# Channel shuffle on one core: eleven tiles of up to 51 KB a partition in two load and two store buffers, in place of fifteen tiles of up to 38 KB in two and three

## The chip, the cores and the metric

The kernel runs on one core of one Trainium2 chip. The metric is the device time of one execution in microseconds. The core has a VectorE (DVE) that copies data inside the on-chip memory (SBUF, 128 partitions), two sequencers that issue transfers here (SP for loads, ACT for stores), and 16 DMA engines that carry them out. The time before is the median of three runs, which lie between 316.12 and 316.22 us.

## The reference

The input x has the shape 16 x 64 x 64 x 256 in float32, 67.1 MB. The 256 channels are 8 groups of 32, and the two channel axes change places at each pixel:

```python
x = x.reshape(batch, h, w, groups, channels_per_group)
x = x.transpose(0, 1, 2, 4, 3)
x = x.reshape(batch, h, w, c)
```

No value is changed. Each pixel's 256 floats (1 KB) are permuted within that kilobyte, so any cut of the data between pixels is allowed.

## The kernel before

All 65,536 pixels lie in one line in memory. A tile is a run of 128 x q pixels: partition p of the tile holds q neighbouring pixels, so q KB a partition, and in DRAM the tile is one contiguous block. The list `_SLOTS` (line 12) gives the tiles' q in order: a tile of 12 that is loaded and stored in two parts of 4 and 8, one of 28, twelve of 38 and one of 16. They sum to 512 KB a partition.

For each tile three things happen. SP issues the load from DRAM into a buffer of the load pool (line 55). VectorE copies the buffer into one of the store pool, reading with a stride so that the channels are permuted (the copy of lines 57 to 60, L57 in the profile). ACT issues the store of that buffer to DRAM (line 61). A tile with two parts has two loads, two copies and two stores.

The order on each engine is the order in which the program is written (the schedule is set to manual in line 43); each engine goes through its own instructions one after another, and semaphores hold an instruction until what it needs is there. Both pools hand out their buffers in turn, each of the size of the largest tile. With two load buffers (line 13), a load waits until the copy of the tile two places back has ended. With three store buffers (line 14), a copy waits until the store of the tile three places back has landed, besides its own load. A store waits for its copy. Buffers take 2 x 38 + 3 x 38 = 190 KB of each partition.

Loads go through one DMA queue (q1 in the profile), stores through another (q10). Each DMA moves one contiguous piece of q KB for each partition, eight pieces on each of the 16 DMA engines.

Of the kernel before, what the change touches and what calls it, by code (L numbers as in the profile page):

```python
# [1 line left out]

# [4 lines left out]


F32 = mybir.dt.float32
P = 128  # L10

_SLOTS = [[4, 8], [28]] + [[38]] * 12 + [[16]]
_IN_BUFS = 2
_OUT_BUFS = 3


@with_exitstack
def kernel(
    ctx: ExitStack,
    tc: tile.TileContext,  # L20
    x: bass.AP,
    groups: bass.AP,
    out: bass.AP,
):
    nc = tc.nc
    b, h, w, c = x.shape
    G = int(groups)
    CPG = c // G
    assert G * CPG == c
    assert sum(map(sum, _SLOTS)) * P == b * h * w  # L30
    biggest = max(map(sum, _SLOTS))

    x_flat = x.rearrange("b h w c -> (b h w c)")
    out_flat = out.rearrange("b h w c -> (b h w c)")

    in_pool = ctx.enter_context(tc.tile_pool(name="in_pool", bufs=_IN_BUFS))
    out_pool = ctx.enter_context(tc.tile_pool(name="out_pool", bufs=_OUT_BUFS))

    def rows(flat, first, q):

        return flat[first * c : (first + P * q) * c].rearrange("(p f) -> p f", p=P)

    ctx.enter_context(tc.manual_schedule(engines=None))
    first = 0
    for parts in _SLOTS:
        in_tile = in_pool.tile([P, biggest * c], F32, name="in_tile")
        out_tile = out_pool.tile([P, biggest * c], F32, name="out_tile")
        at = 0
        pieces = []
        for q in parts:  # L50
            pieces.append((q, first, slice(at * c, (at + q) * c)))
            first += P * q
            at += q
        for q, start, cols in pieces:
            nc.sync.dma_start(out=in_tile[:, cols], in_=rows(x_flat, start, q))  # L55
        for q, start, cols in pieces:
            nc.vector.tensor_copy(  # L57
                out=out_tile[:, cols].rearrange("p (i j g) -> p i j g", j=CPG, g=G),
                in_=in_tile[:, cols].rearrange("p (i g j) -> p i j g", g=G, j=CPG),
            )  # L60
            nc.scalar.dma_start(
                out=rows(out_flat, start, q), in_=out_tile[:, cols]
            )


# [1 line left out]
_INS = ['x', 'groups']  # L67
_OUTS = [((16, 64, 64, 256), 'float32')]

_NUMBERS = {'groups': 8}  # L70


# [26 lines left out]
```

## Time and profile before

| what | value |
|---|---|
| median of three runs | 316.12 us |
| span of the profiled execution | 314.4 us |
| VectorE busy | 119.0 us in 16 copies |
| moved | 67.11 MB read, 67.11 MB written, mean 427 GB/s |
| copy of 38 KB a partition | 8.79 us mean, 12 of them |
| load of 38 KB a partition, issue to landing | 37.0 us median |
| store of 38 KB a partition, issue to landing | 42.6 us median |

A profile shows one execution, taken by the hardware profiler. Its own time, the span, runs from the first to the last instruction; the time of a run also contains what lies around that. The page gives busy times of the engines, then the span in 40 equal slices with the DMA engines' busy share in tenths and the GB/s moved; then the chain of waits that ended last, which is followed back from the last instruction to whatever released each step. Behind each group of instructions stands the idle time of its engine before them and what ended it. "DVE" is VectorE, "SPq" and "ACTq" are the sequencers that issue loads and stores. The latency of a DMA contains the time that it stands in its queue behind others: a 38 KB load moves 4.98 MB.

### The profile page before, as it was taken

What the parts mean: (1) busy time and instruction counts of PE and PEld (TensorE: products, weight loads), DVE (VectorE), ACT (ScalarE), POOL (GpSimd) and SP (SyncE); (2) the same over time, 40 slices, a digit from 0 to 9 for tenths busy, and PEclk for the clock granted to TensorE, in tenths of its full rate; (3) what the DMA queues carried; (4) which work ended last, traced back from release to release, by engine and by line L of the source; (5) the groups of instructions that cost most, each with busy time, mean ns of one, the idle gap of its engine ahead of it and who ended that gap; (6) DMA issues with size and microseconds to landing.
All of it is one profiled execution on the core that took longest, in us unless ns stands there. A gap on an engine that the chain in (4) does not pass through costs nothing.

```text
span 314.4 us, 132 instructions
## 1 busy us (share of the span) xinstructions
DVE 119.0 (38%) x16; POOL 0.2 (0%) x4
## 2 busy tenths in 40 slices
DVE  2081907309109109019028028037046055065400
POOL 0000000000000000000000000000000000000000
DMA  7999999999999999999999999999999999999997
GB/s 317 405 441 416 435 416 483 401 465 406 450 421 446 426 436 436 401 470 396 475 396 475 396 470 401 470 401 470 401 450 421 446 426 436 436 417 450 429 421 321
DMA packets 4608, 134.22 MB, mean 427 GB/s; under 512 B 512, under 2 KB 512, under 8 KB 768
## 3 DMA queue, kind: packets, MB, share of 16 engines
q1 hardware_dynamic: 2304, 67.11, 49.8%
q10 hardware_dynamic: 2304, 67.11, 49.4%
HBM read 67.11 MB, written 67.11 MB: 427 GB/s over the span
## 4 chain that ended last, share of the span: by engine, by line
DMA 76%; DVE 19%; issue 0%; SPq 0%; DVEq 0%
DMA in_tile<-in_x_dram 76%; DVE out_tile L57 19%; SPq L55 0%; DVEq L57 0%
## 5 line engine op out<-in xcount | busy, mean ns | idle before, releaser
L57 DVE COPY out_tile<-in_tile 128x9728 f32<-128x9728 f32 (+4 forms) x16 | 119.0, 7440 | 179.4 <-DMA in_tile<-in_x_dram 179.4
L80 POOL MEMSET const-uint8-127<- 128x1 uint8 x1 | 0.1, 103 | 0.0
L80 POOL MEMSET const-bfloat16-1.0<- 128x1 bf16 x1 | 0.1, 102 | 0.0
L80 POOL MEMSET const-float32-1.0<- 128x1 f32 x1 | 0.1, 100 | 0.0
L80 POOL MEMSET const-float32-0.0<- 128x1 f32 x1 | 0.1, 99 | 0.2 <-issue 0.2
## 6 DMA issues: line engine op xcount, KB each, us to landing
in_tile<-in_x_dram SPq DMA_DIRECT2D x12, 4864.0 KB, 37.0
out_dram<-out_tile ACTq DMA_DIRECT2D x12, 4864.0 KB, 42.6
in_tile<-in_x_dram SPq DMA_DIRECT2D x1, 3584.0 KB, 14.7
out_dram<-out_tile ACTq DMA_DIRECT2D x1, 3584.0 KB, 30.9
in_tile<-in_x_dram SPq DMA_DIRECT2D x1, 2048.0 KB, 30.4
out_dram<-out_tile ACTq DMA_DIRECT2D x1, 2048.0 KB, 15.2
in_tile<-in_x_dram SPq DMA_DIRECT2D x1, 1024.0 KB, 5.4
out_dram<-out_tile ACTq DMA_DIRECT2D x1, 1024.0 KB, 25.0
```

What stands on the lines that cost most here:

```text
L57: nc.vector.tensor_copy(out=out_tile[:, cols].rearrange("p (i j g) -> p i j g", j=CPG, g=G), in_=in_tile[:, cols].rearrange("p (i g j) -> ...
L80: nc = _bacc.Bacc("TRN2", target_bir_lowering=False, num_devices=1)
```

## The change

The list of tiles and the number of store buffers change: one tile of 20 KB a partition, nine of 51 KB and one of 33 KB, no tile in two parts, and two store buffers. The sum is again 512 KB. The buffers grow to 51 KB each, and the two pools take 2 x 51 + 2 x 51 = 204 KB of each partition. There are 11 loads, 11 copies and 11 stores in place of 16 each; a copy waits for the store of the tile two places back. Nothing else is touched.

```diff
-_SLOTS = [[4, 8], [28]] + [[38]] * 12 + [[16]]
+_SLOTS = [[20]] + [[51]] * 9 + [[33]]
 _IN_BUFS = 2
-_OUT_BUFS = 3
+_OUT_BUFS = 2
```

## The prediction

> **What bounds the kernel now.** I read the page first, then DMA shares in windows, the waits, the timeline and the single DMA packet records of the trace. The page:
>
> ```profile
> span 314.4 us, 132 instructions
> DVE 119.0 (38%) x16; POOL 0.2 (0%) x4
> ...
> DMA  7999999999999999999999999999999999999997
> ...
> DMA packets 4608, 134.22 MB, mean 427 GB/s; under 512 B 512, under 2 KB 512, under 8 KB 768
> ...
> DMA in_tile<-in_x_dram 76%; DVE out_tile L57 19%; SPq L55 0%; DVEq L57 0%
> ```
>
> The chain of waits (last line) calls loads 76% and copies 19% of the path. The DMA row above it says more: apart from the first and the last slice the 16 DMA engines are never idle. VectorE is busy for 38%. The chain runs load, copy, load, because a load is issued when a copy frees its buffer; but that load then waits behind another one. So the copies on the chain cost nothing as long as both queues, or at least one, hold work. The windows confirm it (columns: stretch, length, DVE busy, POOL busy, clock, DMA share, GB/s):
>
> ```profile
> 94.00:140.00 46.00, 17.54 (x2) 0.00 (x0) 1.00 1.00 433
> 140.00:186.00 46.00, 17.67 (x2) 0.00 (x0) 1.00 1.00 433
> 186.00:232.00 46.00, 17.59 (x2) 0.00 (x0) 1.00 1.00 433
> 1.70:48.00 46.30, 18.50 (x4) 0.00 (x0) 1.00 1.01 422
> ```
>
> In the middle the share is 1.00 and the rate 433 GB/s, across every border between tiles. 134.22 MB at 433 GB/s are 310.0 us. The packet records run from 1.75 to 313.28 us, 311.5 us. So 1.5 us were lost to slower packets, 1.75 us lie before the first packet and 1.2 us behind the last. These 4.4 us, plus the fixed cost of a DMA, are all that any change of tile sizes can win.
>
> The packets are whole partition rows, eight of a DMA on each DMA engine: 159 ns for 4 KB, 309 for 8, 611 for 16, 1,062 for 28 and 1,439 for 38, a line of 8.8 ns + 37.64 ns per KB; in a chain each starts some 4 ns before the former's recorded end. The two queues take turns, a row of a load and a row of a store, and the small packet that signals a DMA's end (9 ns) takes a turn too: nine turns a DMA.
>
> Of the slower packets, those after 34.6 us sum to nothing. Before, an engine loses 0.29 us in the first packets, 0.16 us (5.2%) while loads of 28 KB rows run alone up to 9.1 us, 0.27 us (1.2%) from 9.1 to 32.5 us where large load rows meet small store rows, and 0.36 us in one row at 33 us: 1.1 us.
>
> The end of the timeline and the wait table of VectorE and the DMA queue of SP:
>
> ```profile
> 278.19 8.73 DVE L57 COPY out_tile<-in_tile 128x9728 f32<-128x9728 f32 x1 [14.21 <-DMA in_tile<-in_x_dram]
> 286.96 11.83 ACTq L61 DMA_DIRECT2D out_dram<-out_tile  x2
> 294.54 3.87 DVE L57 COPY out_tile<-in_tile 128x4096 f32<-128x4096 f32 x1 [7.62 <-DMA in_tile<-in_x_dram]
> ```
> ```profile
> DVE out_tile L57 <- DMA in_tile<-in_x_dram: 179.4, 16, 14.3
> ```
> ```profile
> SPq L55 <- DVE out_tile L57: 106.2, 13, 8.9
> ```
>
> VectorE waits 179.4 us, all of it for loads, never for a store: the third store buffer is not what it waits on. The last load lands at 294.42, the last copy ends at 298.41; the DMA engines spend that time on the store queue's backlog, and the last store's first row goes at 308.0. **This cover of 9.6 us is the place where the change can hurt.**
>
> **The change, part by part.** *Fewer DMAs.* 16 loads, copies and stores become 11 of each; bytes are the same. A DMA costs each engine eight rows' fixed part (8.8 ns by duration, about 4.6 with the overlap) and 9 ns for the signal: 46 to 79 ns. Ten DMAs fewer: -0.46 to -0.79 us. I take -0.5, since in a chain the overlap counts.
>
> [...]
>
> *Rows of 51 KB.* No packet of that size is in the trace. By the line it takes 1,928 ns (1,925 in a chain). The five sizes lie within 2 ns of the line, so I allow +-0.1%, 0.3 us over the run.
>
> *The copies.* From 4,096 to 9,728 elements the mean grows by 0.873 ns an element: 11.70 us for 51 KB, 4.77 for 20 KB, 7.67 for 33 KB. None is on the end's path while a queue has work. A tile's period is 2 x 8 x 1.925 + 0.02 = 30.8 us, so the copy leaves 19 us of play.
>
> *Two store buffers.* A copy now also waits for the store of two tiles back (before: three). ACT's next store is queued behind this copy, and SP's load of two tiles on needs the buffer that the copy empties. By the turn count below the awaited store ends three turns, some 11 us, ahead of the load that the copy needs anyway. Price: 0. If that slack went, the load queue would still hold a queued load for 19 us.
>
> [...] The waits above show none for stores, and the DMA share is 1.00.
>
> *The start.* The first load of 20 KB rows takes 8 x 0.757 = 6.06 us from 1.75, with 0.29 + 0.2 us of slow packets: end at 8.3, landing near 8.7, copy to 13.5, first store issued then. Loads of 51 KB rows run meanwhile, nothing idles. But loads are alone until about 20 us, 18 us instead of 7.3. At the 1.5% seen on 8 KB rows or the 5.2% of the 28 KB rows the additional 10.7 us cost 0.16 to 0.56 us. Mixed rows until 39 us cost about as before; the 0.36 us at 33 us may or may not return. Sum -0.2 to +0.56; I take +0.2.
>
> *The end.* Before, the first store began after 3 rows of the third load: loads were 9 + 9 + 3 = 21 turns ahead of 16 x 9 = 144. At the loads' end the stores had had 123 turns: 13 DMAs and 6 rows, so 2 rows of the fourteenth store were left. The packet records show just 2. There the store was issued at 5.19, so ready near 6.2, with one row of that load started and two more that went ahead of it. After: the first store is issued at 13.5 and ready near 14.6; four rows of the second load have started by then (8.3, 10.2, 12.2, 14.1), and two more make 6: a lead of 9 + 6 = 15 turns of 99. Stores get 84 turns: 9 DMAs and 3 rows, so 5 rows of the last 51 KB store are left, k = 5, or 9.62 us. To cover: 0.4 us to landing, 0.1 to the start of the copy, 7.67 copy, 0.03 to issue, and 1.02 from issue to packet (first load: 0.73 to 1.75), 9.2 us. Margin +0.4 us. One lead row less (k = 4) leaves a hole of 1.5 us, k = 3 one of 3.4. More is likelier than less: store 1 becomes ready near 39 us, just when store 0's last row goes, and each load row that slips in adds one to k. Price 0, with bounds 0 and +3.4.
>
> *Sum.* -0.5 + 0.2 + 0 = -0.3 us: a span of 314.1 us. The profiled run's 314.4 stands 1.7 us under its median of 316.12; the same distance gives **315.8 us**.
>
> **The rivals.**
>
> 1. *The last store comes too late (slower).* Its mechanism is the hole above. For it: the last tile grows from 16 to 33 KB, its copy from 3.87 to 7.67 us, and cover shrinks from 9.6 us to 0.4. Against it: store 1's late start adds rows. It decides once fewer than 4.8 rows of the large store are left at the last load's end: k = 4 gives 315.8 + 1.5 = 317.3, k = 3 319.2. Chance 0.2.
> 2. *Load rows alone are slow (slower).* If 5.2% held for all load-heavy time to 39 us, that is 1.94 us instead of 0.79: with -0.5, +0.65, or 316.8. For it: the 28 KB rows grew from 1,062 to as much as 1,298 ns. Against: the 8 KB rows alone, and everything mixed after 34.6. Chance 0.07.
> 3. *Faster.* If the slow packets fall to the 0.29 at the start, -0.5 - 0.8 = -1.3: 314.8. For it: the single slow row of 0.36 us is tied to nothing that I can see. Against: most of the rest comes in load-heavy time, which grows. Chance 0.15.
> 4. *Two store buffers throttle each tile.* Only if a copy is held over 19 us. Against it: by the turn count the awaited store is 11 us early, each time. If both queues emptied during each copy, nine copies of 11.7 us would lie bare, some 105 us. Chance 0.01.
>
> **How the numbers follow.** About 0.2% (0.63 us) is what a measurement of this kernel can tell from no change: 315.49 to 316.75. The forecast holds 0.57, all of it within that. Faster: 0.15, rival 3. Slower: rivals 1, 2 and 4, 0.28. The range starts at 315.1, inside rival 3, and ends at 317.4 with k = 4; outside remain k = 3, rival 4 and half of rival 3. The likeliest case alone spans 315.5 to 316.4.
>
> **What would show it.** Right: DMA share 1.00 from 40 us to the end, packets of about 1.93 us, VectorE still waiting only for loads, last load near 291 us, and the last store's packets directly behind those of the 51 KB store. Wrong: an idle stretch of the DMA engines behind 300 us (rival 1), a low rate up to 20 us (rival 2), or copies waiting for stores (rival 4).

## The result, and the profile after

The changed kernel takes 370.43 us (median of 4 runs, 369.99 to 371.59), the one before on the same chip 316.14 us (316.12 to 316.22). The ratio is 1.172 (95% interval 1.171 to 1.174). 315.8 us were predicted, between 315.1 and 317.4. The profiled execution has a span of 368.7 us, 54.3 more than before. The granted clock is 1.00 in every run of this document; where the runs of one kernel lie far apart (e2, e5, e13), each time is given.

The head of the page after:

```profile
span 368.7 us, 104 instructions
DVE 219.6 (60%) x11; POOL 0.2 (0%) x4
...
DVE  0507999900994099309930993299139903990960
...
DMA  9989948999999999999999999999999999999958
GB/s 369 431 347 468 398 96 363 357 374 385 380 368 374 357 368 374 368 357 374 351 374 368 368 374 374 385 385 368 363 351 368 391 344 382 329 351 408 431 236 352
...
DVE out_tile L57 40%; DMA out_dram<-out_tile 37%; DMA in_tile<-in_x_dram 8%; SPq L55 0%; DVEq L57 0%
```

Three things are new. VectorE is busy for 219.6 us in place of 119.0, with the same bytes to copy. The DMA engines have a hole in the sixth slice and one near the end. And between the holes, where the share is 9 in every slice from the eighth on, they move some 370 GB/s in place of 433: they are busy, and slow. The chain of waits names copies and stores; before it named loads.

The copies after, grouped by shape (columns: line, engine, operation, shapes, count, busy time and mean ns, idle before):

```profile
L57 DVE COPY out_tile<-in_tile 128x13056 f32<-128x13056 f32 x9 | 200.4, 22274 | 117.0 <-DMA out_dram<-out_tile 101.9 <-DMA in_tile<-in_x_dram 15.1
L57 DVE COPY out_tile<-in_tile 128x8448 f32<-128x8448 f32 x1 | 14.5, 14476 | 9.4 <-DMA out_dram<-out_tile 9.4
L57 DVE COPY out_tile<-in_tile 128x5120 f32<-128x5120 f32 x1 | 4.7, 4749 | 10.3 <-DMA in_tile<-in_x_dram 10.3
```

51 and 33 KB go at 1.706 and 1.714 ns an element, 20 KB at 0.928; the slope between sizes was 0.873 before. The odd pixel counts, 51 and 33, are the slow ones here. Before, every count was even (4, 8, 28, 38, 16).

Windows after (stretch, length, DVE busy, POOL busy, clock, DMA share, GB/s), and below them its wait table for VectorE:

```profile
28.00:40.00 12.00, 9.84 (x1) 0.00 (x0) 1.00 0.97 420
46.00:53.50 7.50, 7.50 (x2) 0.00 (x0) 1.00 0.22 56
60.00:200.00 140.00, 81.43 (x4) 0.00 (x0) 1.00 0.99 370
200.00:340.00 140.00, 89.09 (x4) 0.00 (x0) 1.00 0.99 367
353.20:357.40 4.20, 3.13 (x1) 0.00 (x0) 1.00 0.44 191
```
```profile
DVE out_tile L57 <- DMA out_dram<-out_tile: 111.3, 8, 18.0
DVE out_tile L57 <- DMA in_tile<-in_x_dram: 25.4, 2, 15.1
```

The packet records (one packet is one partition row, or the signal that ends a DMA) split the 54.3 us without a rest. "Line" is what all packets would take by 8.8 ns + 37.64 ns per KB (9 ns for an end signal); each figure is a sum over all packets divided by 16 engines:

```
us per DMA engine            before    after
packets by the line           310.9    310.1
packets above the line          1.1     42.8
idle (span less packets)        2.4     15.8
span                          314.4    368.7
```

So 0.8 us are saved as forecast, 41.7 are lost to slower packets, and 13.4 to idle time. Of the idle time 6.8 us lie between 46 and 53.5 us and 3.0 between 353.2 and 357.4. Slow copies can explain the holes. That they should also slow the packets is not evident; the experiments go after that.

### The profile page after: what moved, and what is told of

The parts are those of the page before. It is cut to its first block, busy times and chain, and to the rows that moved or that the text cites. A ratio compares the mean times of both kernels' runs of the same rounds, so it can differ in the third digit from the quotient of the medians.

```text
span 368.7 us, 104 instructions
## 1 busy us (share of the span) xinstructions
DVE 219.6 (60%) x11; POOL 0.2 (0%) x4
## 3 DMA queue, kind: packets, MB, share of 16 engines
q1 hardware_dynamic: 1584, 67.11, 48.7%
q10 hardware_dynamic: 1584, 67.11, 47.0%
## 4 chain that ended last, share of the span: by engine, by line
DMA 45%; DVE 40%; another core or an unknown queue 11%; issue 0%; SPq 0%; DVEq 0%
DVE out_tile L57 40%; DMA out_dram<-out_tile 37%; DMA in_tile<-in_x_dram 8%; SPq L55 0%; DVEq L57 0%
## 5 line engine op out<-in xcount | busy, mean ns | idle before, releaser
L57 DVE COPY out_tile<-in_tile 128x13056 f32<-128x13056 f32 (+2 forms) x11 | 219.6, 19972 | 136.7 <-DMA out_dram<-out_tile 111.3
```

The costliest lines, as they stand in the source:

```text
L57: nc.vector.tensor_copy(out=out_tile[:, cols].rearrange("p (i j g) -> p i j g", j=CPG, g=G), in_=in_tile[:, cols].rearrange("p (i g j) -> ...
```

## The experiments

### Which part of the change

Four kernels: even tiles (e1), the change with each odd copy in two (e2), the old tiles with two store buffers (e3), and odd rows in the old scheme (e4). In e2 and e4 the copy of an odd number q of pixels becomes one of q - 1 and one of a single pixel.

```diff
e1_even50, against after
-_SLOTS = [[20]] + [[51]] * 9 + [[33]]
+_SLOTS = [[20]] + [[50]] * 9 + [[42]]
e2_split51, against after
+            for part in ([(0, q - 1), (q - 1, q)] if q % 2 else [(0, q)]):
+                at_c = slice(cols.start + part[0] * c, cols.start + part[1] * c)
...
e3_before_2out, against before
-_OUT_BUFS = 3
+_OUT_BUFS = 2
e4_odd_split, against before; copies split as in e2
-_SLOTS = [[4, 8], [28]] + [[38]] * 12 + [[16]]
+_SLOTS = [[4, 8], [28]] + [[37], [39]] * 6 + [[16]]
```

> Tiles 20, nine of 50, 42 KB, all even, two and two buffers: the rows are 2% shorter than 51 KB, the buffers as few, but each copy has an even pixel count. Theory 1 (the copy of an odd number of pixels runs at half speed, and its lateness makes both the holes and the slow packets): copies of 50 KB take 11.5 us, packets 1,891 ns, DMA share 1.00, time 315 to 318 us. Theory 2 (rows of about 50 KB slow each other when loads and stores alternate, whatever the copy does): copies 11.5 us, packets still 10 to 20% over the line, 345 to 362 us. Theory 3 (rows of an odd number of KB are the trouble of the DMA engines): as theory 1 in time.

> The changed kernel's tiles and buffers, but each copy of 51 (33) pixels is made as one of 50 (32) and one of 1. Theory 1: the two copies take 11.5 + 0.4 us, the holes go and so do the slow packets: 315 to 318 us. Theories 2 and 3: the copies are fast and the holes go (some 12 us), but the packets of 51 KB still take 2.2 to 2.3 us while loads and stores alternate: 350 to 360 us.

> The kernel before with two store buffers instead of three, nothing else. If two store buffers alone cost something: copies wait for stores. By the turn count a copy of 38 KB needs the store that ends 5.7 us after its load has landed, so VectorE waits for stores about 5 us a tile; the load queue still holds work, so I expect 316 to 317 us and DMA share 1.00. If store buffers are the cause of the 17%, over 330 us.

> The kernel before with tiles of 37 and 39 KB in turn instead of 38, and copies of 36 + 1 or 38 + 1 pixels: odd rows of the old length, fast copies, two and three buffers. Theory 3 (odd rows): packets 10 to 20% over the line, 340 to 365 us. Theories 1 and 2: packets on the line (1,402 and 1,477 ns), 316 to 317 us.

| kernel | us, median (range) | ratio to before, 95% |
|---|---|---|
| e1_even50 | 320.57 (320.06 to 321.12) | 1.012 (1.010 to 1.015) |
| e2_split51 | 359.76, 357.33, 322.75, 321.24 | 1.018 (1.014 to 1.021) for the two short runs |
| e3_before_2out | 316.11 (316.01 to 316.24) | 0.999 (0.998 to 1.000) |
| e4_odd_split | 316.14 (316.07 to 317.13) | 1.000 (0.999 to 1.001) |

e3 clears the store buffers for the old tiles, although its wait table is turned over:

```profile
DVE out_tile L57 <- DMA out_dram<-out_tile: 168.8, 13, 14.3
DVE out_tile L57 <- DMA in_tile<-in_x_dram: 13.2, 3, 7.7
```

Copies now wait 168.8 us for stores, where before they waited for nothing but loads, and it costs nothing (ratio 0.999): the DMA share is 1.00 to 1.01 from 60 to 300 us. In e4 rows of an odd number of KB (37 and 39) did no harm to the transfers of the old scheme (ratio 1.000). In e1 the copies of 50 KB take some 11.5 us and VectorE 118.0 us in all; the time falls by 50 us. Windows of e1:

```profile
40.00:120.00 80.00, 30.69 (x4) 0.00 (x0) 1.00 1.01 437
...
200.00:290.00 90.00, 34.40 (x3) 0.00 (x0) 1.00 1.00 433
...
300.20:305.00 4.80, 3.98 (x1) 0.00 (x0) 1.00 0.05 21
```

The middle is as fast as before, with 50 KB rows and two store buffers. What e1 still loses is a hole before the last store: the last load lands at 294.42, the last copy of 42 KB runs until 304.18, and the engines have run out of rows at about 300. This is the hole of rival 1 of the prediction, at its place; what makes it is said behind the experiments.

e2 restores the copies of 51 KB (50 pixels 11.44 us, one pixel 0.39 us), but its four runs fall into two pairs, near 322 and near 358 us. The profiled one is of the long pair, and it changes course in the middle. Windows of e2:

```profile
40.00:100.00 60.00, 25.35 (x6) 0.00 (x0) 1.00 1.00 426
100.00:166.00 66.00, 22.73 (x3) 0.00 (x0) 1.00 1.01 429
...
170.00:260.00 90.00, 23.42 (x4) 0.00 (x0) 1.00 0.98 370
```

VectorE does here what it did before 166 us, and yet the rate falls from 429 to 370. At 167.5 us the store queue was empty for a moment. So in this run the packets turn slow without a slow copy; something about the two queues is different afterwards. No short run has a profile, so that the gap is what parts the two pairs is not shown. Rows of 51 KB are odd here too; e8 and e7 below have slow packets with even rows.

### Is a slow copy enough, and what does it do to the queues

e8 takes e1 and splits each 50 KB copy as 49 + 1 pixels; the odd part is slow again (21.70 us for both parts, below). e5 does the same to the old tiles (37 + 1). e6 and e7 tried to put the queues out of step without a slow copy: e3, and behind the fourth tile's load one more load of 8 or 16 partitions of that tile into a buffer that nothing reads.

```diff
e8_slow50, against e1; e5_slow38, against before, with q == 38
+            for part in ([(0, q - 1), (q - 1, q)] if q == 50 else [(0, q)]):
...
e6_dephase8, against e3; e7_shift16 with 0:16
+            if turn == 3:
+                nc.sync.dma_start(
+                    out=extra[0:8, :], in_=rows(x_flat, start, q)[0:8, :]
+                )
```

> The kernel before, each 38 KB copy made as 37 pixels and 1, so at half speed (1.7 ns an element: some 16.2 us); three store buffers. If slow copies by themselves slow the DMA engines: over 330 us. If they do harm only where a queue runs dry: the copy starts when its load lands, and the next load has 23 us, so 16.6 us fit, the backlog of stores shrinks from 19.6 to about 12 us and never to nothing: 316 to 317.5 us.

> The kernel before with two store buffers (316.1 us, as known) and one more load, once, of 8 partitions x 38 KB into a buffer that nothing reads, behind the fourth tile's load: one more row for eight of the DMA engines, none for the others, so that from there on half of the engines are one row behind, load where the others store. Mixing theory (the DMA engines reach 433 GB/s when all load or all store at a time, and lose 10 to 20% when some load while others store): 340 to 365 us, packets of 38 KB up to 2 us. Without such an effect: 0.3 MB more, 316.5 to 317.8 us.

> As the run with 8 more rows, but the additional load has 16 partitions: one row more for every engine, so they stay in step. Mixing theory: 0.6 MB more at 433 GB/s, +1.4 us: 317 to 318 us. If the additional load as such does harm: as slow as the run with 8.

> The run with tiles of 20, nine of 50 and 42 KB (320.6 us), with each 50 KB copy made as 49 pixels and 1, so at half speed (some 21.8 us). If the slow copies are what starts the slow packets in the changed kernel (they leave the queues empty near 46 us, and loads and stores begin again together): 350 to 370 us. If rows of 51 KB are needed for that: only the hole at the start and a longer one at the end are added, 325 to 335 us.

e8 takes 367.46 us (367.32 to 368.94), ratio 1.163 (1.161 to 1.166). One line of its timeline on VectorE, and two of its windows:

```profile
90.98 21.70 DVE L59 COPY out_tile<-in_tile 128x12544 f32<-128x12544 f32 x2 [17.68 <-DMA out_dram<-out_tile]
```
```profile
28.00:40.00 12.00, 10.00 (x1) 0.00 (x0) 1.00 0.98 422
60.00:200.00 140.00, 80.48 (x9) 0.00 (x0) 1.00 1.00 373
```

Slow copies alone turn 320.6 us into 367.5, with even tiles. But the copy did not slow a packet by running beside it: from 28 to 40 us after, while the first slow copy runs (30.16 to 52.43), the single packets of 51 and 20 KB lie on the line (1,928 and 761 ns, all of them).

e5 missed its expectation: 341.46, 343.23 and 342.53 us in three of its four runs and 318.83 in one, in place of some 317. Copies of 38 KB at half speed take 16.2 us and leave play in a period of 23 us, and three store buffers are there. In its profile, of a long run, the rate is 416 to 419 GB/s from 40 to 118 us and 396 to 400 from 125 us on; the change again comes with a gap in the queues, at about 120 us.

e6 (329.98 us, 329.28 to 333.89; ratio 1.046, 1.040 to 1.052) was the test of the theory of that moment, that packets slow down where some engines load while others store. Part of its trace refutes it: between 60 and 120 us eight engines load while eight store, at 434 GB/s. e7 (331.37 us, 331.25 to 331.48; ratio 1.048, 1.047 to 1.050) missed by 13 us: its engines are in step and its copies fast, and yet from 105 to 300 us it goes at 411 GB/s, its stores of 38 KB some 0.15 us above the line. Behind its extra load, from 55 to 85 us, it still goes at 436 GB/s.

What e7, e5, e2, e8 and the changed kernel have in common while they are slow shows in the order of packets on one DMA engine: the end signals of a load and of a store come together. (The records name a packet's queue but not its engine. A packet is put here behind the one whose recorded end lies some 4 ns after its start, which gives 16 chains; a few packets could go into either of two.) Each DMA gives an engine eight rows and an end signal (the page of after has 1,584 packets for 11 loads, nine for each of 16 engines), so where both end together, store row r follows load row r. That row r of each DMA lies in the same partitions is an assumption; no record shows it.

### The same row numbers, or something else

The next kernels set other causes against this. e11 changes the order in which tiles are taken, so that loads and stores are elsewhere in DRAM. e9 stores partitions 64 to 127 ahead of 0 to 63, so that by this assumption rows at the same turn lie in other partitions. e12 is e7 with three extra loads, which should carry the row numbers past each other. e13 is e1 with the last tile in two, to mend its end.

```diff
e9_upper_first, against after
+            for lo in (64, 0):
+                nc.scalar.dma_start(
+                    out=rows(out_flat, start, q)[lo : lo + 64, :],
+                    in_=out_tile[lo : lo + 64, cols],
+                )
e11_other_order, against after
+_ORDER = [0, 1, 6, 2, 9, 4, 8, 3, 7, 5, 10]
e12_shift48, against e7
+            for again in range(3 if turn == 3 else 0):
...
e13_even_tail, against e1
-_SLOTS = [[20]] + [[50]] * 9 + [[42]]
+_SLOTS = [[20]] + [[50]] * 9 + [[26]] + [[16]]
```

> The changed kernel with each store issued as two, partitions 64 to 127 first, then 0 to 63. In all slow runs so far (the changed kernel; even tiles with slow copies; 38 KB with slow copies; the load of 16 more rows) the end signals of a load and of a store fall together on each DMA engine, so that row r of a load alternates with row r of a store, of the same partition of both buffers; in the fast ones they are a row or more apart. Same-partition theory: now they differ, the 51 KB packets return to 1.93 us, the holes of the slow copies stay: 322 to 338 us. If the packets are slow for another reason (slow copies on VectorE, row length): 365 to 375 us.

> The changed kernel, its tiles taken in another order (0, 1, 6, 2, 9, 4, 8, 3, 7, 5, 10), so that the distance in DRAM between the load and the store that alternate is another for each pair, while partitions fall together as before. Same-partition theory: 366 to 374 us, as the changed kernel. If the fixed distance of the two in DRAM makes the packets slow: at most some pairs are slow, 325 to 355 us.

> The kernel before with two store buffers and three more loads of 16 partitions x 38 KB in place of one (331.4 us): 1.9 MB more than with none, 1.3 MB more than with one. One such load moved the loads' ends by two turns, just onto the stores' ends; three move them six turns, past them. Same-partition theory: fast again in spite of more bytes: 316.1 + 4.4 = 320.5, within 319.5 to 324 us. If the additional loads do harm as such: 335 to 360 us.

> The changed kernel's idea without its two faults: tiles of 20, nine of 50, 26 and 16 KB, all even, two and two buffers. Against the run with 42 KB at the end (320.6 us) the last copy takes 3.9 us instead of 9.6, so the hole of 4.9 us before the last store goes. If that hole is all that separates it from the kernel before: 315.4 to 316.6 us. If long rows or few buffers cost more: 318 to 321 us.

e11: 369.9 us (369.67 to 371.81), ratio 1.171 (1.168 to 1.174), the same as after. So the particular distances in DRAM are not the cause. They are still whole numbers of 51 KB tiles, as in the changed kernel, so e11 by itself does not clear every relation of addresses. The end of after says more: from 305 to 339 us its store rows of 51 KB follow load rows of 33 KB with the same number, whose distance in DRAM is another for each partition (18 KB more from one to the next, if equal numbers are equal partitions), and these 121 store rows lie 605 ns above the line, more than the others.

e9 could tell nothing: 411.94 us (406.92 to 414.69), because its stores became slow by themselves. At the end of its profile, where half-partition stores go alone, the median row of 51 KB takes 4.07 us in place of 1.93.

e12: 331.83 us (331.78 to 331.88), ratio 1.050 (1.048 to 1.051), over the 319.5 to 324 expected. The stretch with the extra loads is where it loses: 159 to 330 GB/s in three slices of the page from 49.5 to 74 us. Behind them its windows answer the question that it was made for:

```profile
71.00:120.00 49.00, 11.66 (x2) 0.00 (x0) 1.00 1.00 432
120.00:180.00 60.00, 23.70 (x3) 0.00 (x0) 1.00 1.01 435
...
240.00:300.00 60.00, 18.35 (x3) 0.00 (x0) 1.00 1.00 431
```

The same extra buffer and the same kind of load as e7, but store rows that are 2 to 6 numbers from the load row ahead of them: no 38 KB row off the line, 431 to 435 GB/s.

e13 missed: 320.94, 321.96, 320.48 us and one run of 361.83, in place of about 316. The long last copy alone is not what held e1 up. In the trace most engines end their loads by 300.5 us, but three are some 3 us and two some 7 us behind, so the last load lands at 307.58 and the last store starts after a hole up to 312.6. The run of 361.83 has no profile; that it is of the kind of e2's long pair is a guess from its time.

### The test by cause: 8 KB that move the turn order

With e3 as the base the store's row numbers lie 1 or 2 behind the load's. One additional DMA on the load queue takes two turns of each engine if it has one row for each: the row and the end signal. A load of 16 partitions x 512 bytes is such a one, 8 KB in all and 27 ns a row by its packet records (the load queue of e16 has 2,336 packets in place of e3's 2,304, two more for each engine); it should put row upon row (e16). In the changed kernel the same load should take them apart (e14), and one of 128 partitions, nine turns, should be a control that leaves them as they are (e15). Each reads into a buffer that nothing else reads.

```diff
e16_before_two_turns, against e3; e14_two_turns, against after; e15_nine_turns, against after, with 0:128
+    extra = extra_pool.tile([P, 128], F32, name="extra")
...
+            if turn == 3:
+                nc.sync.dma_start(
+                    out=extra[0:16, :], in_=rows(x_flat, start, q)[0:16, 0:128]
+                )
```

> The changed kernel with one additional load, once, behind the fourth tile's load: 16 partitions x 512 bytes (8 KB in all), one tiny row and one end signal for each DMA engine, two turns. Same-row theory (a store's row is slow when it follows the load row of the same number, so of the same partition): from about 92 us on the loads' rows stand one row behind the stores', the packets return to 1.93 us and a tile to 30.9 us instead of 36.3: 368.7 - 7 x 5.4 = 331 us span, 326 to 340 us as a time. If the row number has nothing to do with it: 368 to 372 us.

> As the run with two turns, but the additional load has 128 partitions x 512 bytes: eight tiny rows and a signal, nine turns, a whole DMA's worth, so that the loads and stores that follow stand as before, row on row. Same-row theory: 366 to 372 us. If any small transfer in between frees the queues: as fast as the run with two turns.

> The kernel before with two store buffers (316.1 us) and the same 8 KB load of 16 partitions behind the fourth tile's load. There the loads stand two turns off the stores by one such step, as the run with 16 rows of 38 KB showed (411 GB/s, 331.4 us, of which some 4 us for its own bytes). Same-row theory: rows now fall on each other in a kernel whose copies, tiles and bytes are those of 316 us: 325 to 329 us, the stores' packets near 1.57 us. Otherwise 316 to 316.5 us.

e16 takes 328.05 us (327.97 to 328.22), ratio 1.036 (1.034 to 1.039), as expected. One stretch of one DMA engine in the packet records of e3 and of e16 (L and S: a row of a load or a store with its KB, l# and s#: the end signals, @ start in us, [ns] where a packet is more than 30 ns off the line):

```
e3   L38@113.5 S38@115.0 l# @116.4 S38@116.4 L38@117.9 S38@119.3 L38@120.7 s# @122.2 L38@122.2 S38@123.6
e16  L38@116.6 S38@118.1[1578] L38@119.7 S38@121.1[1621] l# @122.7 s# @122.7 L38@122.7 S38@124.2[1582]
```

Windows of e3, then of e16:

```profile
60.00:120.00 60.00, 20.19 (x3) 0.00 (x0) 1.00 1.01 436
120.00:180.00 60.00, 26.38 (x3) 0.00 (x0) 1.00 1.01 436
```
```profile
60.00:120.00 60.00, 18.06 (x3) 0.00 (x0) 1.00 1.01 412
120.00:180.00 60.00, 25.55 (x3) 0.00 (x0) 1.00 1.00 408
```

In e3 the load's signal comes two row pairs ahead of the store's; in e16 both come together, and nearly every store row is slow (96% of those counted below are over 100 ns off) while the load rows stay on the line. The sum fits: the 1,536 store rows of 38 KB average 1,562 ns in place of 1,439, and (1,562 - 1,439) x 1,536 / 16 engines = 11.8 us, against 11.9 us between the medians. An 8 KB load costs 12 us here, and what it moves is the turn order. Its buffer of 512 bytes a partition may also shift the buffers behind it; that this alone makes packets slow is answered by e14 below, which has the same buffer and goes at 433 GB/s for a while.

In most traces the slow store rows sort by one quantity, the store row's number less the number of the load row just ahead of it on its engine (rows that follow a load row of their own size, between 60 and 300 us, for e12 from 71 us):

```
kernel              rows KB   offset              mean over the line, ns
before, e3            38      -2                    0
e12                   38      -6 to -4, 2 to 4      0
e7, e16               38       0                 +128, +153
e5, e6                38       0                  +91, +88
e1                    50       2, 3                 0
e2, up to 168 us      51       2, 0                +4, +439 (56 rows at 0)
e14                   51       2, 0                 0, +221
after, e8          51, 50      0                 +240, +279
```

Single end signals are missing in the records, so that a few offsets are counted by rows alone. In after one in fifteen of the 51 KB store rows stands at -1 or 1, and these are slow as well (+273 and +271 ns). At 51 KB only 53% of the rows at 0 are over 100 ns off; at 38 KB 96% of e16's and 79% of e7's are, and no row at another offset in e3 or e12 is. Two traces have both kinds of engine at one time: in e6 from 120 to 200 us eight engines at 0 average 20 to 150 ns over the line while the other eight, at -2, have next to no slow row, and in e14 from 150 to 195 us five engines at 0 average 93 to 326 ns while nine at 2 have none.

**Equal numbers are not enough, however.** In e7 all 160 store rows of 38 KB from 55 to 85 us stand at 0, end signals together, and none is more than 15 ns off the line; from 85 us on they turn slow, engine by engine. In e6 the same eight engines stand at 0 from 60 to 110 us with 130 such rows, none over 8 ns off. In e7 and e16 the 128 store rows of 38 KB that follow 16 KB load rows of the same number, near 300 us, lie on the line. So a slow store row of 38 KB stands at 0, but a row at 0 need not be slow; what else it takes, these runs don't show.

e14 took 359.58 us (358.56 to 361.19), ratio 1.137 (1.132 to 1.142), in place of 326 to 340. Its windows show the repair work and then be lost:

```profile
108.00:150.00 42.00, 28.71 (x2) 0.00 (x0) 1.00 1.00 433
150.00:240.00 90.00, 57.52 (x3) 0.00 (x0) 1.00 1.00 406
250.00:340.00 90.00, 53.76 (x3) 0.00 (x0) 1.00 0.94 356
```

With store rows two numbers ahead of the load rows it goes at 433 GB/s, 22 us copies or not. From 150 us on five engines, and later six to eight, stand at equal numbers again and are slow. Near 248 us a queue is dry, both restart together, and most engines have equal numbers from then on. e15 (361.84 us, 360.14 to 362.73; ratio 1.143, 1.138 to 1.147) was no clean control: its nine small turns passed while eight store rows did, so that it too went at 431 GB/s from 120 to 148 us, until the ends fell together from about 150 us on.

### Can a version beat both?

With even tiles, small tiles at both ends and two store buffers the change could still win a little.

```diff
e17_small_start50, against after
+_SLOTS = [[4, 8], [28]] + [[50]] * 9 + [[22]]
e18_small_start46, against after
+_SLOTS = [[4, 8], [28]] + [[46]] * 10 + [[12]]
```

> Two and two buffers of 50 KB, all tiles even, but the small tiles of the kernel before at the start: 4 + 8, 28, nine of 50, 22 KB. In the runs with 20 KB first and 50 KB behind, one or a few DMA engines fell some 4 to 7 us behind the others in the first 30 us, which made the last load land late and left a hole of 4.9 us (320.6 and 321.5 us). If the small tiles are what keeps the engines in step and the loads' rows two off the stores': 315.6 to 316.8 us. If long rows lose the step by themselves: 319 to 322 us, with some runs far above.

> The same with ten tiles of 46 KB and 12 KB at the end: 14 transfers each way instead of 16, two and two buffers. Fixed costs of two transfers each way, some 0.2 us, are saved: 315.7 to 316.4 us if rows and engines stay in step; 318 us and more if not.

e17: 318.27 us (317.89 to 318.8), ratio 1.006 (1.005 to 1.008). e18: 316.9 us (316.19 to 317.81, 12 runs), ratio 1.002 (1.001 to 1.003). Neither beats before; e3 and e4 equal it. Both go at 432 to 434 GB/s from 60 to 280 us. By the packet records the profiled e17 (span 316.2) saves 0.5 us by the line, loses 0.6 to slower packets and idles 3.0 us behind 308 us, where before idles 1.4: its engines don't end together. e18's profiled execution (315.8) idles 2.8 us there.

## Why the prediction was wrong

**"The copies."** This is the step that failed first: "From 4,096 to 9,728 elements the mean grows by 0.873 ns an element: 11.70 us for 51 KB, 4.77 for 20 KB, 7.67 for 33 KB." The 20 KB copy measured 4.75 us, the others 22.27 and 14.48. The line was drawn through even pixel counts and applied to odd ones. e2 (11.44 + 0.39 us for 50 + 1 pixels) and e8 (21.7 us for 49 + 1, where e1 takes 11.5 for 50) show that it is the odd pixel count and not the size: 1.71 ns an element for 51 pixels against 0.90 for 50. Why an odd count is slow, no run shows.

**"None is on the end's path while a queue has work", "the copy leaves 19 us of play".** The condition was right and the copy broke it. At the start the play was smaller still: the second load lands at 30.1 us, the rows of the third are through at about 46, and the next load and the next store both wait for the copy that ends at 52.43. The 6.8 idle us between follow. Rival 4 put its threshold at a copy that is held over 19 us; here no wait held it, it was 22.3 us long by itself. The queues did not empty during each copy, as that rival priced: from 60 to 340 us the DMA share is 0.99, and the holes come at the start and at the end alone.

**"Rows of 51 KB. ... By the line it takes 1,928 ns".** Right for a row that is not on top of another: most of the loads alone in the first 16 us, and the stores alone from 338 to 352 us, take 1,928 ns. Over the whole run the mean is 2,252 ns for loads and 2,179 for stores. "I allow +-0.1%" had no room for a state of the two queues that the trace of before never shows. This is the larger part, 41.7 of 54.3 us. That it follows from the first is shown by e1 and e8, which differ in the copies alone. The way it does so fits the trace: the copy's end releases a load and a store at one moment; they enter two empty queues together, and from then on finish together (the load at 92.37 and the store at 92.54 us, 128.46 and 128.63, 165.07 and 165.24), which releases the next pair together again.

**"Two store buffers. ... Price: 0".** Right by itself (e3: ratio 0.999), and also at 50 KB in e1's middle. The waits that rival 4 named do appear (111.3 us), but e3 has more of them at no cost: waiting was not the price here. The 13.4 us of idle engines and the 41.7 us of slower packets were.

**The start.** +0.2 us was taken, at most +0.56. By the packet records the packets up to 40 us lie 1.57 us above the line after and 1.53 in e1, which starts the same way with fast copies, in place of 1.12: some +0.4, inside the bound. Rival 2, with +1.15, did not come true. The first copy after starts at 10.30 us in place of the 8.7 that were reckoned with: 15 engines end the first load at 8.1 to 9.1 us, one at 10.0.

**The end.** The margin of +0.4 us was below nothing: the hole of rival 1 is there after (3.0 us idle, where the last copy takes 14.48 us in place of 7.67) and in e1 (4.3 us idle with a 42 KB copy of 9.64 us). In e1 the count's assumption that all engines are in step is what fails: the last load waits for an engine that is some 6 us behind the others (294.42 us, the others up to 288.55).

**Fewer DMAs.** By the line -0.8 us, the far end of the -0.46 to -0.79 that were given, and swallowed by the rest.

What stays open. That slow copies cost the 47 us between e1 and e8, and that a shift of the turn order alone costs 12 us in e16, is shown. That slow store rows go with equal row numbers is shown at 38 KB; that equal numbers are the whole reason is refuted by e7 up to 85 us and e6 up to 110. That the partition which a read and a write then share has to do with it is an inference, and e9, which should have told, could not; the fast rows at equal numbers speak against it as the only condition. Why loads become slow too from 50 KB on (a mean of 2,252 ns after, +0.32 us), while 38 KB loads stay on the line in e16, is not known, nor why single engines fall behind with 50 KB tiles. A third store buffer of 51 KB wasn't tried.

## What to carry to other kernels

When a tile size changes, read off what it does to the pixel count of the VectorE copy: here 33, 37 and 51 pixels took 1.71 ns an element (14.48, 16.21 and 22.27 us), 20 and 50 pixels 0.93 and 0.90, so a line through even counts did not hold for odd ones. Where loads and stores share saturated DMA engines, look at the packet order as well as at the share: here a share of 0.99 with 370 GB/s in place of 433 meant slower packets, and they came while load and store end signals fell together, though not always then. Try to keep the queues from running dry at the same moment: what restarted together at 52 us in the changed kernel stayed together for the rest of the run.

## What the runs showed of the hardware that wasn't expected

- The packet time went with the turn order of two full queues. Store rows that follow the load row of the same number averaged 0.13 to 0.15 us more at 38 KB in e7 and e16 and 0.24 to 0.28 us at 50 and 51 KB, so that the queues moved 411 or 370 GB/s in place of 433; but in e7 160 such rows in a line were at full speed. In e16 one 8 KB DMA that shifted the turns cost 12 us.
- Large rows of two transfers over part of the partitions were slow: the median 4.07 us for 51 KB where 64 partitions are stored in e9, beside 1.93. In e6 one 38 KB load row on each of the 16 engines takes 4.2 to 4.8 us at the time of the 8-partition load, beside 1.44; only eight of them can be its own. Why is not shown.
- Identical runs of one program can take two courses, 322 and 358 us in e2. In the long run that was profiled, the rate fell behind a short gap in one queue.
